# Squares of the attention sub-norm written to an SBUF tile instead of a PSUM bank, and seven statistics tiles with two buffers instead of three

## The chip, the cores and the metric

The kernel runs on one core of one Trainium2 chip. The metric is the device time of one execution in microseconds (us); less is better. Five engines run their own instruction streams, each in order, and meet at semaphores: TensorE (PE: matmuls and transposes, into PSUM), VectorE (DVE), ScalarE (ACT), GpSimd (POOL, which has no PSUM operand in this kernel) and SyncE (SP, which issues DMAs).

## The reference

A two-layer encoder over 1040 positions (1024 tokens and 16 meta tokens) with 1024 channels. Each layer computes, with `rms_norm(x, g) = x * rsqrt(mean(x*x) + eps) * g`:

```
h = rms_norm(h_res, norm_gain[li])
f_in, q, k, v, gate = split(h @ w_in[li])
f_out = real(fft2(f_in per group)) @ w_fourier          # 4 groups of 128 channels
q, k = rotary(rms_norm(q)), rotary(rms_norm(k))         # 4 heads, two maps of 64 channels each
o = (softmax(q0 k0) - lam * softmax(q1 k1)) @ v         # per head, 128 channels
o = rms_norm(o, subln_gain[li]) * (1 - lambda_init)     # the attention sub-norm
h_res = h_res + (concat(f_out, o) * silu(gate)) @ w_out
```

The sub-norm needs, for each position and head, the sum of the squares of 128 numbers. It is this sum that the change touches most.

## The kernel before, in words

All large products are split into a high and a low part (F32R), so one product takes three matmuls. A layer has four stages: the Fourier group (`fourier`, lines L352 to L450), the projection of head 0, attention, and the output projection (`out_fourier`, `phase_out`, matmuls of L286). Attention on one head needs little TensorE time beside its waits, so the projections of heads 1 to 3 (matmuls of L547) and later the output projection (L286) run inside it as a filler: a generator from which `fill(n)` takes steps.

Attention runs over 4 heads and, in each, 4 groups of query tiles: two tiles of 128 rows, in the last group of layer 0 also the 16 meta rows. For one tile (an item):

- `scores`: matmuls of L635 and L637 write the scores of one of the two maps into S, a PSUM tile of three banks of which there is one. DVE L642 copies the scores to SBUF (tile p) and finds the row's extreme, ACT L645 takes the exponential and its sum. The same for the second map. DVE L653 combines the two.
- `transposes`: eight transposes (L663, four to a bank) and one small one for the 16 meta columns (L670, a third bank) turn p around. ACT L667 and L673 copy the result out of PSUM, DVE L668 and L674 subtract to get the low part.
- `values`, after a group's last item: 25 matmuls (L682, L683) into one bank, copied to the SBUF tile osb by ACT L685.
- `finish`, one item later: TensorE transposes osb into a bank (L696, tile `pb`), ACT L698 copies it back over osb (`ot` is a view of osb), ACT L703 squares `ot` with the row scale r1 and sums the squares into `so`, writing the squares themselves back into the bank `pb`. DVE L705, POOL L707 (power -1/2) and DVE L708 make the row factor, DVE L710 multiplies it and the gate into gt, and SP sends it off.

The banks `pb` of `transposes`, `values`, `finish`, and those for keys (L587) and queries (L614), all come from one pool M of three PSUM banks (`psM`, tag "M"); S takes three banks and the pool G, for projections, two, which makes eight. A bank is free for its next user when the last instruction that reads or writes it is done. The squares of L703 are never read; only their sums are.

`wl`, the low part of a weight block, is made by POOL (in part by DVE) at L184 from the staged weights wst and the high part wh (ACT, L182).

The order of instructions on each engine is not that of the code: a list scheduler, with its own timing of the chip, orders them when the kernel is built, gives each tile a buffer of its pool and puts in the semaphore waits. `fill` sets the filler's priority below that of the attention work.

Of the kernel before, what the change touches and what calls it, by code (L numbers as in the profile page):

```python
# [10 lines left out]
F32 = mybir.dt.float32  # L11
F32R = mybir.dt.float32r
AF = mybir.ActivationFunctionType
# [5 lines left out]
P = 128  # L19
# [31 lines left out]
def trunk(ctx: ExitStack, tc, x, meta, ngain, w_in, w_f, qg, kg, lq1, lk1, lq2, lk2, subg, w_out,  # L51
          ident_d, chan_d, rope_d, dft_d, dftt_d, out, dbg=None):
    nc = tc.nc
    pe, act, dve, pool, sp = nc.tensor, nc.scalar, nc.vector, nc.gpsimd, nc.sync
# [4 lines left out]
    sm = ctx.enter_context(tc.tile_pool(name="sm", bufs=3))  # L59
# [7 lines left out]
    def nm(s):  # L67
        uid[0] += 1
        return f"{s}_{uid[0]}"
# [28 lines left out]
    def tile_rows(t):  # L98
        return NMETA if t == NT else P
# [113 lines left out]
    def norm_tile(hT, hM, gb, xt, t, wk, inplace=False):  # L213
        R, pos = tile_rows(t), P * t
        xn = wk.tile([P, D], F32, tag="xn", name=nm("xn"), bufs=1 if inplace else 2)
        ssq = sm.tile([P, 1], F32, tag="ssq", name=nm("ssq"))
        act.activation(xn[0:R], xt[0:R], AF.Square, accum_out=ssq[0:R])
        ms = sm.tile([P, 1], F32, tag="ms", name=nm("ms"))
        dve.tensor_scalar(ms[0:R], ssq[0:R], 1.0 / D, EPS, op0=ALU.mult, op1=ALU.add)
        rs = sm.tile([P, 1], F32, tag="rs", name=nm("rs"))  # L220
        pool.tensor_tensor(rs[0:R], ms[0:R], nhalf[0:R, 0:1], op=ALU.pow)
        if inplace:
            xn = xt
        dve.scalar_tensor_tensor(xn[0:R], xt[0:R], rs[0:R], gb[0:R], op0=ALU.mult, op1=ALU.mult)
        for c in range(2):
            pb = bank()
            for j in range(4):
                k = 4 * c + j
                pe.transpose(pb[:, R * j:R * j + R], xn[0:R, P * k:P * k + P], ident[0:R, 0:R])
            src = pb[:, 0:4 * R].rearrange("p (k r) -> p k r", k=4)  # L230
            hi = hT[:, 4 * c:4 * c + 4, 0, pos:pos + R]
            lo = hT[:, 4 * c:4 * c + 4, 1, pos:pos + R]
            act.copy(hi, src)
            dve.tensor_tensor(lo, src, f(hi), op=ALU.subtract)
            if t == NT:
                for o, part in ((0, hi), (32, lo)):
                    act.copy(hM[:, 4 * c:4 * c + 4, o:o + R], f(part))
# [218 lines left out]
    def head_projection(li, h, hT, hM, ep, wk, store, w, nxt, progress):  # L456
# [7 lines left out]
        ss = None  # L464

        def evacuate(t, ps, a, kv):
            nonlocal ss
            R = tile_rows(t)
            with tc.high_priority(EVAC):
                if t == NT:  # L470
                    pm = [ep.tile([P, 256], F32, tag="sq", name=nm("pm"), bufs=3) for _ in range(2)]
                    for part, u, v in ((pm[0], a, 256), (pm[1], 256, 384 if kv else 512)):
                        part = part[0:R, u % 256:(v - 1) % 256 + 1]
                        act.copy(part, ps[32:32 + R, u:v])
                        dve.tensor_tensor(part, ps[0:R, u:v], part, op=ALU.add)
                    pqk, pvg = pm[0], pm[1]
                else:
                    pqk, pvg = ps[:, 0:256], ps[:, 256:512]
                if not kv:
                    gs = ep.tile([P, P], F32, tag="gs", name=nm("gs"), bufs=2)  # L480
                    act.activation(gs[0:R], pvg[0:R, P:2 * P], AF.Tanh, scale=0.5)
                    dve.scalar_tensor_tensor(gs[0:R], gs[0:R], 1.0, pvg[0:R, P:2 * P], op0=ALU.add, op1=ALU.mult)
                act.copy(qk[0:R, t, a:256], pqk[0:R, a:256])
                sq = ep.tile([P, 256], F32, tag="sq", name=nm("sq"), bufs=3)
                act.activation(sq[0:R, a:256], pqk[0:R, a:256], AF.Square)
                act.copy(va[0:R, t, :], pvg[0:R, 0:P])
            if not kv:
                sp.dma_start(gtd[li][h][t, 0:R, :], gs[0:R])
            if t % 3 == 0:
                ss = sm.tile([P, 12], F32, tag="ss", name=nm("ss"))  # L490
            c0, c1 = 4 * (t % 3) + a // HD, 4 * (t % 3) + 4
            if t == NT:
                pool.memset(ss[:, 4 * (t % 3):c1], 1.0)
            dve.tensor_reduce(ss[0:R, c0:c1], sq[0:R, a:256].rearrange("p (c d) -> p c d", d=HD), axis=AX.X,
                              op=ALU.add)
            if t % 3 == 2:
                t0 = t - 2
                reg = qk[:, t0:t0 + 3, :]
                dve.tensor_scalar(ss, ss, 1.0 / HD, EPS, op0=ALU.mult, op1=ALU.add)  # L499
                rs = sm.tile([P, 12], F32, tag="rsq", name=nm("rsq"))  # L500
                pool.tensor_tensor(rs, ss, nhalf[:, 0:12], op=ALU.pow)  # L501
                n12 = reg.rearrange("p t (c d) -> p (t c) d", d=HD)
                dve.tensor_tensor(n12, n12, rs.unsqueeze(2).to_broadcast([P, 12, HD]), op=ALU.mult)
                n5 = reg.rearrange("p t (i c d) -> p (t i) c d", i=2, d=HD)

                def tab(x, lo, hi):
                    y = x[:, t0:t0 + 3, :, lo:hi].rearrange("p t i d -> p (t i) d")
                    return y.unsqueeze(2).to_broadcast([P, 6, 2, hi - lo])

                r1 = ep.tile([P, 256], F32, tag="sq", name=nm("r1"), bufs=3)  # L510
                r2 = ep.tile([P, 256], F32, tag="sq", name=nm("r2"), bufs=3)
                r1 = r1[:, 0:12 * ROT].rearrange("p (t c d) -> p t c d", t=6, c=2)
                r2 = r2[:, 0:12 * ROT].rearrange("p (t c d) -> p t c d", t=6, c=2)
                dve.tensor_tensor(r1, n5[:, :, :, 0:ROT], tab(cgt, 0, 16), op=ALU.mult)
                dve.tensor_tensor(r2[:, :, :, 0:8], n5[:, :, :, 8:16], tab(sgt, 0, 8), op=ALU.mult)
                dve.tensor_tensor(r2[:, :, :, 8:16], n5[:, :, :, 0:8], tab(sgt, 8, 16), op=ALU.mult)
                dve.tensor_tensor(n5[:, :, :, 0:ROT], r1, r2, op=ALU.add)
                progress[h] = t // 3 + 1
                if t == NT and ("qk", li, h) in dbg:
                    sp.dma_start(dbg["qk", li, h], qk)  # L520
# [35 lines left out]
    def attention(li, wk, store, fill, marks, ready, progress):  # L556
# [131 lines left out]
        def finish(h, gi, osb, ls):  # L688
            sets = [(0, 2, P)] + ([(2, 1, NMETA)] if len(group_tiles(gi)) > 2 else [])
            for i0, n, R in sets:  # L690
                t0 = group_tiles(gi)[i0]
                gt = wk.tile([P, 2, P], F32, tag="gt", name=nm("gt"), bufs=1)
                sp.dma_start(gt[0:R, 0:n], gtd[li][h][t0:t0 + n, 0:R, :].rearrange("t p d -> p t d"))
                pb = bank()
                for i in range(n):
                    pe.transpose(pb[0:R, P * i:P * i + P], osb[:, P * (i0 + i):P * (i0 + i) + R], ident)  # L696
                ot = osb[:, 0:2 * P].rearrange("p (t d) -> p t d", t=2)
                act.copy(ot[0:R, 0:n], pb[0:R, 0:P * n].rearrange("p (t d) -> p t d", t=n))  # L698
                r1 = sm.tile([P, 2], F32, tag="r1", name=nm("r1"))
                dve.reciprocal(r1[0:R, 0:n], ls[0:R, i0:i0 + n])  # L700
                so = sm.tile([P, 2], F32, tag="so", name=nm("so"))
                for i in range(n):
                    act.activation(pb[0:R, P * i:P * i + P], ot[0:R, i], AF.Square, scale=r1[0:R, i:i + 1],  # L703
                                   accum_out=so[0:R, i:i + 1])
                dve.tensor_scalar(so[0:R, 0:n], so[0:R, 0:n], 1.0 / P, EPS, op0=ALU.mult, op1=ALU.add)  # L705
                rs = sm.tile([P, 2], F32, tag="rso", name=nm("rso"))
                pool.tensor_tensor(rs[0:R, 0:n], so[0:R, 0:n], nhalf[0:R, 0:n], op=ALU.pow)  # L707
                dve.tensor_tensor(rs[0:R, 0:n], rs[0:R, 0:n], r1[0:R, 0:n], op=ALU.mult)  # L708
                for i in range(n):
                    dve.scalar_tensor_tensor(gt[0:R, i], ot[0:R, i], rs[0:R, i:i + 1], gt[0:R, i],  # L710
                                             op0=ALU.mult, op1=ALU.mult)
                    sp.dma_start(yad[li][t0 + i][0:R, P * h:P * h + P], gt[0:R, i])
                    if h == NH - 1:
                        ready.add(t0 + i)
# [29 lines left out]
        for n, item in enumerate(items):  # L744
            h, gi, i, t = item
# [107 lines left out]
    with tc.tile_pool(name="in0", bufs=2, side="right", reuse_waits="tile") as wk:  # L853
        for t in list(range(MT)) + [NT] + list(range(MT, NT)):
            R = tile_rows(t)
# [9 lines left out]
    for li in range(DEPTH):  # L865
# [9 lines left out]
        acm, wk = open_pool(f"at{li}", far, 2)  # L875
# [125 lines left out]
```

## Time and profile before

| | us |
|---|---|
| median of 3 runs | 1237.96 (1237.94 to 1243.18) |
| profiled execution, its own time | 1239.06 |
| its span on the page | 1236.9 |
| TensorE busy (matmuls) | 1169.6 (95%) |
| VectorE busy | 832.9 (67%) |
| ScalarE busy | 647.4 (52%) |
| GpSimd busy | 262.8 (21%) |
| the two attention stretches, about | 215 to 620 and 845 to 1210 |

The profile is of one execution; its own time lies 1.1 us above the median. Busy time says how long an engine had an instruction running; idle time before an instruction is put down to the engine and line whose end released it (`DVE atl L668`: the VectorE instruction of line 668 that writes atl). Where an instruction waits for several, the one that ended last is named.

### The profile page before, as it was taken

How to read it: one execution, taken by the hardware profiler on the slowest of the kernel's cores; microseconds unless marked ns; L12 is line 12 of the kernel's file. 1: busy time of each engine (PE TensorE's matmuls, PEld its weight loads, DVE VectorE, ACT ScalarE, POOL GpSimd, SP SyncE). 2: the span in 40 equal slices, each digit the busy share in tenths (PEclk: the TensorE clock that was granted, in tenths of full speed). 3: DMA queues.
4: the chain of work that ended last, by engine and by line, in shares of the span. 5: the costliest groups of instructions: out<-in, count | busy, mean ns of one | idle time of the engine just before them, and what ended most of it. 6: DMA issues, size and time to landing. Idle time of an engine off the chain costs nothing.

```text
span 1236.9 us, 18756 instructions
## 1 busy us (share of the span) xinstructions
PE 1169.6 (95%) x6676; PEld 1000.8 (81%) x6676; DVE 832.9 (67%) x1793; ACT 647.4 (52%) x1588; POOL 262.8 (21%) x231
## 2 busy tenths in 40 slices
PE   6999899989998998999999999999999999999998
PEld 6999786877777776778879998877878887878786
DVE  6352435777778778887775244557768888898863
ACT  6232325566657667566453323344667666766631
POOL 5111216023212213011012103252142121211200
PEclk9999899999999999999999999999999999999999
DMA  7420203012002004644436111120020020265353
GB/s 227 136 69 35 73 27 99 7 30 75 12 18 82 16 25 147 187 148 130 147 113 197 54 34 55 59 80 26 16 82 22 28 73 25 82 225 162 109 162 114
DMA packets 103612, 105.46 MB, mean 85 GB/s; under 512 B 11232, under 2 KB 87584, under 8 KB 103264
## 3 DMA queue, kind: packets, MB, share of 16 engines
q1 hardware_dynamic: 103104, 99.59, 25.9%
q0 software_dynamic: 416, 4.70, 1.1%
q8 instruction: 52, 0.85, 0.3%
q14 instruction: 40, 0.33, 0.1%
HBM read 74.62 MB, written 29.62 MB: 84 GB/s over the span
## 4 chain that ended last, share of the span: by engine, by line
PE 66%; DVE 12%; DMA 7%; ACT 6%; issue 5%; POOL 2%; SPq 1%; POOLq 0%; ACTq 0%; DVEq 0%
PE G L547 20%; PE G L286 10%; PE G L352 7%; PE S L352 6%; PE M L682 5%; PE S L635 4%; PE S L637 3%; PE S L547 3%; DVE p L642 3%; PE M L663 2%; PE M L393 2%; DMA wst<-in_w_in_dram 2%; ACT p L645 2%; DVE p L653 1%; DMA xt<-in_x_dram 1%
## 5 line engine op out<-in xcount | busy, mean ns | idle before, releaser
L547 PE MATMUL G<-wh,hT 128*128 128x512 f32 x896 | 308.7, 404 | 4.7 <-ACT wh L182 2.5
L645 ACT ACTIVATE p<-p,mx 128x1040 f32<-128x1040 f32 x136 | 158.4, 1165 | 99.7 <-DVE p L642 96.6
L547 PEld LDWEIGHTS G<-wh,hT 128*128 128x128 f32 x896 | 169.2, 190 | 44.6 <-ACT wh L182 3.4
L642 DVE TENSOR_SCALAR_CACHE_REDUCE p<-S 128x1040 f32<-128x1040 f32 x136 | 167.8, 1234 | 33.0 <-PE S L637 28.4
L547 PE MATMUL G<-wl,hT 128*128 128x512 f32 x448 | 178.2, 399 | 1.8 <-POOL wl L184 1.8
L184 POOL TENSOR_TENSOR wl<-wst,wh 128x512 fp32r<-128x512 f32 x82 | 112.6, 1384 | 235.7 <-ACT wh L182 131.1
L286 PE MATMUL G<-wh,yh 128*128 128x512 f32 (+2 forms) x276 | 107.8, 404 | 3.6 <-DVE xt L293 2.3
L182 ACT CAST wh<-wst 128x512 fp32r<-128x512 f32 x128 | 75.0, 620 | 65.0 <-DMA wst<-in_w_in_dram 22.2
L286 PE MATMUL G<-wl,yh 128*128 128x512 f32 (+2 forms) x276 | 106.6, 395 | 0.0
L501 POOL TENSOR_TENSOR rsq<-ss,nhalf 128x12 f32<-128x12 f32 x24 | 58.4, 2433 | 219.4 <-DVE ss L499 190.8
L547 PEld LDWEIGHTS G<-wl,hT 128*128 128x128 f32 x448 | 85.3, 190 | 18.1 <-POOL wl L184 2.8
L352 PE MATMUL G<-hT,wh 128*128 128x384 f32 (+3 forms) x384 | 96.4, 332 | 0.0
L286 PE MATMUL G<-wh,yl 128*128 128x512 f32 (+1 forms) x260 | 93.4, 400 | 0.0
L668 DVE TENSOR_TENSOR atl<-M,ath 128x512 fp32r<-128x512 f32 x136 | 87.0, 656 | 8.0 <-ACT ath L667 6.9
L352 PE MATMUL S<-hT,wh 128*128 128x256 f32 (+3 forms) x384 | 90.7, 320 | 1.0 <-DVE sg L440 1.0
L653 DVE SCALAR_TENSOR_TENSOR p<-p,cc,p 128x1040 f32<-128x1040 f32 (+1 forms) x68 | 89.2, 1312 | 1.5
L637 PE MATMUL S<-k,ql 128*128 128x264 f32 (+3 forms) x408 | 87.3, 321 | 0.0
L667 ACT CAST ath<-M 128x512 fp32r<-128x512 f32 x136 | 73.8, 561 | 22.0 <-PE M L663 21.2
L707 POOL TENSOR_TENSOR rso<-so,nhalf 128x2 f32<-128x2 f32 (+1 forms) x36 | 25.3, 702 | 273.6 <-DVE so L705 256.5
L663 PE MATMUL M<-ident,p 128*128 128x128 f32 x544 | 74.2, 270 | 7.4 <-ACT M L703 3.5
L184 DVE TENSOR_TENSOR wl<-wst,wh 128x512 fp32r<-128x512 f32 x46 | 44.4, 966 | 47.6 <-ACT wh L182 47.3
L663 PEld LDWEIGHTS M<-ident,p 128*128 128x128 f32 x544 | 61.6, 140 | 15.4 <-ACT M L703 4.4
(193 smaller groups left out, 2542.1 us busy)
## 6 DMA issues: line engine op xcount, KB each, us to landing
wst<-in_w_in_dram SPq DMA_DIRECT2D x64, 192.0 KB, 2.8
xt<-in_x_dram SPq DMA_DIRECT2D x16, 512.0 KB, 3.9
wst<-in_w_in_dram SPq DMA_DIRECT2D x32, 256.0 KB, 3.6
wst<-in_w_out_dram SPq DMA_DIRECT2D x16, 512.0 KB, 4.0
xmid<-xt SPq DMA_DIRECT2D x16, 512.0 KB, 3.3
xt<-xmid SPq DMA_DIRECT2D x16, 512.0 KB, 4.3
tab<-in_dft_dram POOLq DMA_DIRECT2D x2, 2096.0 KB, 10.0
yfd<-sg SPq DMA_DIRECT2D x8, 520.0 KB, 2.7
```

The costliest lines, as they stand in the source:

```text
L182: act.copy(h, self.staged[q][:, j, :])
L184: eng.tensor_tensor(l, self.staged[q][:, j, :], f(h), op=ALU.subtract)
L286: pe.matmul(pb[0:m, 0:e - c], lhsT=a[:, k, 0:m], rhs=b[2 * k + n][:, c:e], start=k == 0 and i == 0, stop=k == 3 and i == n_pass - 1)
L352: pe.matmul(o, lhsT=w[k][:, c:c + P], rhs=hT[:, k, s, a:b], start=k == 0 and i == 0, stop=k == KT - 1 and i == 2)
L547: pe.matmul(pss[t][0:part.shape[-1], a:b], lhsT=part, rhs=w[k][:, a:b], start=k == 0 and i == 0, stop=k == KT - 1 and i == len(pairs) - 1)
L637: ins = pe.matmul(ps[0:R, C0 + a:C0 + b], lhsT=ql[:, qo:qo + R], rhs=kk[:, a:b], start=False, stop=True)
L642: dve.tensor_scalar(pc[0:R], ps[0:R, C0:C0 + L], -1.0, None, op0=ALU.mult, op1=ALU.min, accum_out=mx[0:R])
L645: act.activation(pc[0:R], pc[0:R], AF.Exp, bias=mx[0:R], scale=-1.0, accum_out=lc)
L653: dve.scalar_tensor_tensor(pp[0][0:R], pp[1][0:R], cc[0:R], pp[0][0:R], op0=ALU.mult, op1=ALU.add)
L663: pe.transpose(pb[:, R * j:R * j + R], pa[0:R, P * kt:P * kt + P], ident[0:R, 0:R])
L667: act.copy(hi, src)
L668: dve.tensor_tensor(atl[:, 4 * c:4 * c + 4, qo:qo + R], src, f(hi), op=ALU.subtract)
```

## The change

The squares of the sub-norm go to a new SBUF tile `sqo` of 128 by 128 numbers with one buffer. The bank `pb` of `finish` is then last touched by the copy of L698. Seven small statistics tiles (ssq, ms, rs, ss, rsq, so, rso) are given two buffers where they had three. Lines after 701 move down by one: L703 becomes L704.

```diff
@@ norm_tile
-        ssq = sm.tile([P, 1], F32, tag="ssq", name=nm("ssq"))
+        ssq = sm.tile([P, 1], F32, tag="ssq", name=nm("ssq"), bufs=2)
         act.activation(xn[0:R], xt[0:R], AF.Square, accum_out=ssq[0:R])
-        ms = sm.tile([P, 1], F32, tag="ms", name=nm("ms"))
+        ms = sm.tile([P, 1], F32, tag="ms", name=nm("ms"), bufs=2)
         dve.tensor_scalar(ms[0:R], ssq[0:R], 1.0 / D, EPS, op0=ALU.mult, op1=ALU.add)
-        rs = sm.tile([P, 1], F32, tag="rs", name=nm("rs"))
+        rs = sm.tile([P, 1], F32, tag="rs", name=nm("rs"), bufs=2)
@@ evacuate, in head_projection
-                ss = sm.tile([P, 12], F32, tag="ss", name=nm("ss"))
+                ss = sm.tile([P, 12], F32, tag="ss", name=nm("ss"), bufs=2)
...
-                rs = sm.tile([P, 12], F32, tag="rsq", name=nm("rsq"))
+                rs = sm.tile([P, 12], F32, tag="rsq", name=nm("rsq"), bufs=2)
@@ finish, in attention
-                so = sm.tile([P, 2], F32, tag="so", name=nm("so"))
+                so = sm.tile([P, 2], F32, tag="so", name=nm("so"), bufs=2)
+                sqo = wk.tile([P, P], F32, tag="sqo", name=nm("sqo"), bufs=1)
                 for i in range(n):
-                    act.activation(pb[0:R, P * i:P * i + P], ot[0:R, i], AF.Square, scale=r1[0:R, i:i + 1],
+                    act.activation(sqo[0:R], ot[0:R, i], AF.Square, scale=r1[0:R, i:i + 1],
                                    accum_out=so[0:R, i:i + 1])
...
-                rs = sm.tile([P, 2], F32, tag="rso", name=nm("rso"))
+                rs = sm.tile([P, 2], F32, tag="rso", name=nm("rso"), bufs=2)
```

The scheduler makes another order of it. Up to the first `finish` of layer 0 all engines have the order of before. From there on the orders part, mostly inside layer 0's attention, in short pieces. Three places follow; a number behind a tile's name tells its copies apart, and the brackets name the engines whose semaphores a row waits for.

ScalarE in the first `finish`, before (osb_2373 is the group's output, M_2398 the bank of `finish`, M_2437, M_2444 and M_2451 those of the next item's transposes):

```order
L698 COPY osb_2373<-M_2398 128x256 [waits PE_49,Activation_49]
L667 CAST ath<-M_2437 128x4x128 [waits PE_49]
L667 CAST ath<-M_2444 128x4x128 [waits PE_49]
L703 ACTIVATE M_2398,so_2404<-osb_2373,r_342_2402 128x128 [waits Activation_49] x2
L673 CAST att<-M_2451 16x128 [waits PE_49]
L673 CAST att<-M_2451 16x128
```

and after:

```order
L698 COPY osb_2373<-M_2398 128x256 [waits PE_49,Activation_49]
L667 CAST ath<-M_2438 128x4x128 [waits PE_49]
L667 CAST ath<-M_2445 128x4x128 [waits PE_49]
L704 ACTIVATE sqo_2405,so_2404<-osb_2373,r_342_2402 128x128 [waits Activation_49]
L673 CAST att<-M_2452 16x128 [waits PE_49]
L673 CAST att<-M_2452 16x128
L704 ACTIVATE sqo_2405,so_2404<-osb_2373,r_342_2402 128x128 [waits Activation_49]
```

The squares write sqo, and the copies of the small transpose (L673) stand between the two of them.

TensorE around the second `finish` of layer 0, before (M_2678, M_2685 and M_2692 are the three banks of one item's transposes):

```order
L663 MATMUL M_2678<-ident,p_2497 128x128 [waits DVE_49]
L663 MATMUL M_2678<-ident,p_2497 128x128 x3
L635 MATMUL S_2736<-k_2058,qa_2532 128x264 [waits DVE_49]
L635 MATMUL S_2736<-k_2058,qa_2532 128x512
L635 MATMUL S_2736<-k_2058,qa_2532 128x264
L637 MATMUL S_2736<-k_2058,ql_2027 128x264
L637 MATMUL S_2736<-k_2058,ql_2027 128x512
L637 MATMUL S_2736<-k_2058,ql_2027 128x264
L663 MATMUL M_2685<-ident,p_2497 128x128 [waits DVE_49]
L663 MATMUL M_2685<-ident,p_2497 128x128 x3
L670 MATMUL M_2692<-ident,p_2497 16x128 [waits DVE_49]
```

and after:

```order
L663 MATMUL M_2680<-ident,p_2498 128x128 x4
L635 MATMUL S_2738<-k_2058,qa_2533 128x264 [waits DVE_49]
L635 MATMUL S_2738<-k_2058,qa_2533 128x512
L635 MATMUL S_2738<-k_2058,qa_2533 128x264
L637 MATMUL S_2738<-k_2058,ql_2027 128x264
L637 MATMUL S_2738<-k_2058,ql_2027 128x512
L637 MATMUL S_2738<-k_2058,ql_2027 128x264
L663 MATMUL M_2687<-ident,p_2498 128x128 [waits DVE_49]
L663 MATMUL M_2687<-ident,p_2498 128x128 x3
L670 MATMUL M_2694<-ident,p_2498 16x128 [waits Activation_49]
```

The order is the same, but the small transpose L670 waits for ScalarE and no longer for VectorE.

TensorE where the projection of head 2 of layer 0 begins, before (wh and wl are the two parts of its weight block, G_3055 and G_3058 the bank):

```order
L635 MATMUL S_2921<-k_2059,qb_2533 128x264
L637 MATMUL S_2921<-k_2059,ql_2028 128x264
L637 MATMUL S_2921<-k_2059,ql_2028 128x512
L637 MATMUL S_2921<-k_2059,ql_2028 128x264
L683 MATMUL M_2855<-att,vt 128x256 [waits DVE_49]
L547 MATMUL G_3055<-wh_2810,hT_150 128x512 [waits Activation_49]
L547 MATMUL G_3055<-wl_2811,hT_150 128x512 [waits Pool_49]
L547 MATMUL G_3055<-wh_2810,hT_150 128x512
```

and after:

```order
L663 MATMUL M_2784<-ident,p_2629 128x128 [waits DVE_49]
L663 MATMUL M_2784<-ident,p_2629 128x128 x3
L547 MATMUL G_3058<-wh_2812,hT_150 128x512 [waits DVE_49,Activation_49]
L547 MATMUL G_3058<-wl_2813,hT_150 128x512 [waits Pool_49]
L547 MATMUL G_3058<-wh_2812,hT_150 128x512
```

The first matmuls with the new weights stand one item earlier: before the two blocks of scores (S_2888 and S_2924), the small transpose of that item and the 24 value matmuls that precede them in the order of before.

## Rows read from the trace of the kernel before

**Rows 1.** The page, part 1: engine busy time, share of the span, instructions.

```profile
PE 1169.6 (95%) x6676; PEld 1000.8 (81%) x6676; DVE 832.9 (67%) x1793; ACT 647.4 (52%) x1588; POOL 262.8 (21%) x231
```

**Rows 2.** Chain that ended last, in order of time: start, length, what.

```profile
291.52 5.55 PE G L547 x24
```

**Rows 3.** Waits, whole span: who waited for whom, total, times, longest (us).

```profile
PE M L670 <- DVE atl L668: 9.5, 6, 3.2
PE M L670 <- ACT M L703: 9.3, 8, 2.0
...
PE S L635 <- DVE p L642: 4.5, 7, 1.4
...
PE M L663 <- ACT M L703: 3.5, 3, 1.7
...
ACT xn L217 <- DVE ms L219: 0.6, 1, 0.6
```

**Rows 4.** Timeline, first `finish`, all engines: start, length, instruction [idle before <- releaser].

```profile
251.63 0.35 ACT L698 COPY osb<-M 128x256 f32<-128x256 f32 x1
...
251.88 0.64 PE L637 MATMUL S<-k,ql 128*128 128x264 f32 x3
...
253.43 1.28 DVE L668 TENSOR_TENSOR atl<-M,ath 128x512 fp32r<-128x512 f32 x2
253.69 0.19 ACT L703 ACTIVATION_READ_ACCUMULATOR M<-osb,r 128x1 f32 x1
...
253.93 0.28 PE L670 MATMUL M<-ident,p 128*16 128x128 f32 x1 [1.41 <-ACT M L703]
...
254.70 1.23 DVE L642 TENSOR_SCALAR_CACHE_REDUCE p<-S 128x1040 f32<-128x1040 f32 x1
...
254.87 0.70 POOL L707 TENSOR_TENSOR rso<-so,nhalf 128x2 f32<-128x2 f32 x1 [23.88 <-DVE so L705]
```

**Rows 5.** Timeline of TensorE: five small transposes that waited.

```profile
276.80 0.29 PE L670 MATMUL M<-ident,p 128*16 128x128 f32 x1 [3.17 <-DVE atl L668]
...
355.45 0.28 PE L670 MATMUL M<-ident,p 128*16 128x128 f32 x1 [0.73 <-DVE atl L668]
...
476.01 0.28 PE L670 MATMUL M<-ident,p 128*16 128x128 f32 x1 [1.60 <-ACT M L703]
...
905.58 0.28 PE L670 MATMUL M<-ident,p 128*16 128x128 f32 x1 [1.24 <-DVE atl L668]
...
974.07 0.28 PE L670 MATMUL M<-ident,p 128*16 128x128 f32 x1 [0.48 <-ACT M L703]
```

**Rows 6.** Timeline of ScalarE, second `finish` of layer 0.

```profile
273.48 0.37 ACT L698 COPY osb<-M 128x256 f32<-128x256 f32 x1
...
274.70 0.40 ACT L703 ACTIVATE M<-osb,r 128x128 f32<-128x128 f32 x1
```

**Rows 7.** TensorE by stretch: length, busy (instructions), granted clock, DMA share, GB/s.

```profile
276.00:281.00 5.00, 4.20 (x12) 0.66 0.26 70
...
573.90:580.00 6.10, 6.09 (x21) 0.72 0.19 26
```

**Rows 8.** By stretch: length; PE, PEld, DVE, ACT, POOL busy; clock; DMA.

```profile
140.00:480.00 340.00, 317.35 (x1738) 259.60 (x1739) 243.36 (x561) 197.23 (x503) 79.51 (x67) 0.98 0.14 41
```

**Rows 9.** Groups by form: busy us, mean ns | idle before, releasers.

```profile
L182 ACT CAST wh<-wst 128x512 fp32r<-128x512 f32 x128 | 75.0, 620 | 65.0 <-DMA wst<-in_w_in_dram 22.2 <-PE G L352 18.4 <-PE G L547 11.3
...
L703 ACT ACTIVATE M<-osb,r 128x128 f32<-128x128 f32 x64 | 24.2, 378 | 1.3
...
L789 ACT ACTIVATE yh<-G,sgc 128x512 fp32r<-128x512 f32 x16 | 10.9, 683 | 16.8 <-PE G L785 16.5
...
L600 ACT CAST vh<-va 128x1024 fp32r<-128x1024 f32 x8 | 8.4, 1049 | 4.7 <-PE M L682 4.7
```

**Rows 10.** Timeline of TensorE where head 2's projection begins after the change.

```profile
286.46 0.71 PE L635 MATMUL S<-k,qa 128*128 128x264 f32 x3
```

**Rows 11.** Timeline of GpSimd: seventh low part of head 2's weights.

```profile
287.01 1.29 POOL L184 TENSOR_TENSOR wl<-wst,wh 128x512 fp32r<-128x512 f32 x1 [2.01 <-ACT wh L182]
```

## The prediction

> **What bounds the kernel now.** I read the page first. TensorE is busy for 1169.6 us of a span of 1236.9 [rows 1], and the chain that ended last runs through long stretches of its matmuls, such as 24 of L547 in 5.55 us, 0.23 us each [rows 2]. There is no other engine near it: in the larger part of layer 0's attention VectorE is busy for 243.4 of 340 us, 72% [rows 8]. So time is to be won almost only in the 67 us (1236.9 - 1169.6) in which TensorE stands still, and where its clock is granted below full.
>
> The list of waits says what it stands still for. Three entries have to do with the pool M of three banks: L670, the small transpose that takes an item's third bank, waited 9.3 us in 8 places for the squares L703 and 9.5 us in 6 places for VectorE's L668; L663 waited 3.5 us in 3 places for L703 [rows 3]. These 22.3 us are a third of all idle time of TensorE.
>
> The timeline of the first `finish` shows the mechanism. ScalarE has copied the bank out at 251.98 (251.63 + 0.35). TensorE ends its scores at 252.52 and wants the bank for L670, but gets it at 253.93, when the second square is read out (253.69 + 0.19) [rows 4]. It waited 1.41 us for squares that nobody reads.
>
> **The change part by part.** *The bank.* With the squares in SBUF the bank is free after L698. At the first `finish` that is 251.98, half a microsecond before TensorE comes: the wait goes whole. Of the 12.8 us (9.3 + 3.5) that end with L703 I take off two places, 1.60 and 0.48 us [rows 5], since in the new order L670 there waits for VectorE; what it costs there is open. 10.7 us are left.
>
> In four places the old order let L670 wait for L668, and the new one lets it wait for ScalarE: 3.17, 0.73 twice (once at 454.87) and 1.24 us, 5.9 in all [rows 5]. The order of the second `finish` shows it. TensorE came there at 273.63 (276.80 - 3.17) and L698 ended at 273.85 (273.48 + 0.37) [rows 6], so about 0.2 us of the 3.17 stay. Removable together: 10.7 + 5.9, or 16.6 us.
>
> How much of it holds is not in the trace. TensorE comes earlier, but VectorE does not where it works without a gap: after the first `finish` it goes from L668 (to 254.71) straight into L642 at 254.70 [rows 4], and L642 feeds the exponential whatever TensorE does. What then comes late is the next L635, which needs S from L642; it already waits 4.5 us in 7 places [rows 3]. If everything holds, 16.6 us; if VectorE set the pace wherever the two meet, nothing. I take two thirds, 11.1 us, nearer the upper end because VectorE has 28% of its time free in that stretch [rows 8].
>
> *The clock.* In two stretches the granted clock is below full: 0.66 on the mean over 5 us from 276, and 0.72 over 6.1 us from 573.9 [rows 7], a mix of the two levels of 1.2 and 2.4 GHz. Right before the first TensorE had stood still for 3.17 us [rows 5], right before the second for the longest wait for L703, 2.0 us [rows 3]. The lost time is 5 x 0.34 + 6.1 x 0.28 = 1.7 + 1.7 = 3.4 us. Both waits go, so I take 3.4 us back; 0 if something else makes TensorE pause there.
>
> *The squares themselves.* ScalarE's form from SBUF to SBUF with a scale and 128 columns is not in the trace. The form as it stands (to PSUM) takes 378 ns. From SBUF to SBUF a cast of 512 columns takes 620 and one of 1024 columns 1049, or 0.84 ns a column; 128 columns would be 620 - 384 x 0.84 = 298 ns without a scale. The form with a scale from PSUM to SBUF takes 683 at 512 columns, so 361 at 128 [rows 9]. Between 298 and 378 ns, 68 squares change by -5.4 to 0 us on an engine that is 58% busy (197 of 340 us [rows 8]). I take 361 and a value of 0 for the path, since the squares no longer hold a bank.
>
> The Trainium skill, page "ScalarE: Activation LUTs", section "Step-by-step: what each stage is for", says the opposite of a free move: ScalarE writes faster to PSUM than to SBUF, and PSUM is the destination to choose unless TensorE needs most of it. The page gives no figure. The two casts and the scaled form above do not bear the rule out for this size, and its own exception (TensorE needs the banks) is the case here.
>
> *The two squares of a pair* now write one tile, sqo, one after the other. Both rows wait for their own engine in the old order too, so this costs nothing.
>
> *Seven tiles with two buffers.* The next writer must now wait for the reader of two uses before instead of three. For `so` that reader is POOL L707, which ended at 255.57 (254.87 + 0.70) [rows 4], while the next squares come at 274.70 [rows 6]: 19 us of room, and POOL had idled 23.88 us for its input. For ssq the whole list has one wait of 0.6 us [rows 3]. I take 0; at worst such a wait stands once for each of the seven tiles on the path, 4 us.
>
> *The new order.* The scheduler shifts some short pieces, and each can make TensorE meet a thing that isn't ready. The clearest is the start of head 2's projection, one item earlier. In the old trace that place in the program is 286.46, where the item's scores begin [rows 10]; 19 matmuls at 0.23 us [rows 2] and one block of scores (1.0 us) lead from there to the first matmul with the seventh low part, so TensorE asks for it at 291.9, or at 287.5 if it has gained the 1.4 and 3.0 us of the two `finish` before. The low part is ready at 288.30 (287.01 + 1.29) [rows 11]: a wait between 0 and 0.8 us. There are six such weight blocks inside attention, three in a layer. I charge each at 0.6, near the upper end: 3.6 us.
>
> Sum: 11.1 + 3.4 - 3.6 = 10.9 us. From the profiled execution's 1239.06 us that gives 1228.2; the median of the runs is 1.1 lower, so 1227.
>
> **The rivals.**
> - *Taken back.* VectorE and ScalarE set the pace in the item of a `finish`, and the next wait for L642, L653 or L668 grows by most of what went. For it speaks VectorE's gapless run from 253.43 to 255.93 [rows 4]; against it that its 28% of free time lies in between. A third of the 16.6 stays, one of the two clock falls goes, and the new order costs its 3.6: 5.5 + 1.7 - 3.6 = 3.6, so 1234.
> - *Longer squares.* Writing to SBUF takes ScalarE longer than writing to PSUM. Priced with the largest step between two forms of 512 columns, 683 - 620 = 63 ns [rows 9], 68 squares are 4.3 us, all of it on the path if the second cast L667 waits behind them: 1227 + 4.3, or 1231. The forms of rows 9 speak against it. (It is what the rule of the Trainium skill named above would do.)
> - *Weights too late: slower.* TensorE runs ahead of ScalarE's and POOL's weight parts at all six blocks. Where it asks before the cast of the last part has begun, it waits for a whole cast and a whole subtraction, 0.62 + 1.29 = 1.9 us [rows 9, 11], and that pause, as long as the one before 573.9, brings a clock fall of 1.7 with it: 6 x 3.6 = 21.6 us, against 11.1 + 3.4 won. That ends 7.1 us above, at 1245. Four blocks would eat the gain, and all six are needed before it can be told from no change. Against it: POOL idles four fifths of its time [rows 1] and would move up with TensorE, whose matmuls free its wl buffers.
> - *The bank is not the last to come.* L698 itself stands in ScalarE's queue behind an exponential, and L670 finds the bank no earlier: 1238. Against it stand L698's ends at 251.98 and 273.85, before or within 0.2 us of TensorE's coming [rows 4 to 6].
>
> **How the numbers follow.** Forecast 0.60 (1219 to 1233), taken back 0.24, longer squares 0.05, slower 0.07, bank not last 0.04. If all 18.7 us (12.8 + 5.9) and the clock came back with no new wait it would be 1237.96 - 22.1 = 1216. The range of 1219 to 1240 leaves out the best of this and the slower rival. Half a percent, 6.2 us, is about what can be told from no change here: faster means below 1231.8 and takes nearly all of the forecast, the better part of the longer squares and the lucky edge of "taken back", 0.64; slower 0.07; the rest 0.29.
>
> **What would show it.** In the profile of the changed kernel no wait of TensorE for the squares' line (now L704) may be left; waits of L670 and L663 for L698 should be below 1 us in all; those of L670 for L668 fall from 9.5 to about 4. The granted clock is full around 276 and 574. The squares take 340 to 380 ns. TensorE's busy time falls by the 3.4 us or so, its idle time by 7 to 8. If L635's wait for L642 (4.5) grows by as much as the others shrink, it was taken back; if waits of L547 or L286 for wl or wh grow past 10 us, the new order decided. The forecast is wrong if the bank waits are gone and the time is still above 1233.

## The result, and the profile after

The changed kernel takes 1223.17 us, the median of four runs (1219.01 to 1224.20), against 1239.51 for the kernel before (four runs); the ratio is 0.9865, with a 95% interval of 0.9845 to 0.9884. Run again with the second group of experiments, it took 1219.20 against 1239.11, ratio 0.9835 (0.9808 to 0.9862). It is faster by 16 to 20 us, where 10.9 were forecast; both medians lie inside the range of 1219 to 1240, 4 and 8 us below the 1227 us that were forecast. Of all executions of this document one alone, the profiled one of pool_qcopy, ran at a mean granted clock of 0.849 in place of some 0.99, in 1294.63 us, and it is left out of the medians.

The profiled execution took 1219.01 us, 20.05 less than the profiled one of before, so the two profiles lie further apart than the medians. Part 1 of the page of the changed kernel:

```profile
span 1217.2 us, 18766 instructions
...
PE 1163.7 (96%) x6676; PEld 998.2 (82%) x6676; DVE 834.8 (69%) x1793; ACT 645.2 (53%) x1588; POOL 265.2 (22%) x231
```

TensorE stands still for 53.5 us (1217.2 - 1163.7) in place of 67.3 [rows 1]: 13.8 us less, where 7 to 8 were forecast. Its busy time fell by 5.9 us with the same 6676 instructions. That goes with the granted clock: its mean is 0.991 in the profile of before and 0.997 in this one. The list of waits of the changed kernel (waiting instruction, releaser, total us, times, longest):

```profile
PE M L670 <- DVE atl L668: 6.6, 6, 1.4
PE S L635 <- DVE p L642: 4.1, 7, 0.9
...
PE M L229 <- DVE hT L234: 2.6, 3, 1.5
PE G L547 <- ACT wh L182: 2.6, 2, 1.7
PE G L547 <- ACT va L486: 2.5, 2, 2.2
PE G L547 <- POOL wl L184: 1.8, 2, 0.9
...
PE M L663 <- ACT osb L698: 0.5, 2, 0.2
...
PE M L670 <- ACT osb L698: 0.4, 2, 0.2
```

No entry names the squares any more. Their 12.8 us [rows 3] have become 0.9 us for the copy L698, the last reader of the bank now, and the waits of L670 for L668 went from 9.5 to 6.6. L635's wait for L642, where the time would have shown if VectorE had taken it back, went from 4.5 to 4.1. The timeline of the changed kernel shows the first two `finish` (start, length, engine, instruction, [idle before <- releaser]):

```profile
249.23 0.35 ACT L698 COPY osb<-M 128x256 f32<-128x256 f32 x1
...
249.49 0.63 PE L637 MATMUL S<-k,ql 128*128 128x264 f32 x3
...
249.95 0.27 PE L670 MATMUL M<-ident,p 128*16 128x128 f32 x1
...
250.44 0.42 ACT L704 ACTIVATE sqo<-osb,r 128x128 f32<-128x128 f32 x1
...
251.03 0.69 DVE L668 TENSOR_TENSOR atl<-M,ath 128x512 fp32r<-128x512 f32 x1
...
251.36 0.40 ACT L704 ACTIVATE sqo<-osb,r 128x128 f32<-128x128 f32 x1
...
251.63 1.23 DVE L642 TENSOR_SCALAR_CACHE_REDUCE p<-S 128x1040 f32<-128x1040 f32 x1
...
270.75 0.28 PE L670 MATMUL M<-ident,p 128*16 128x128 f32 x1 [0.17 <-ACT osb L698]
```

L670 follows the scores without idle time (249.95) where it had waited 1.41 us, and in the second `finish` it waits 0.17 in place of 3.17 [rows 4, 5]. It now runs ahead of both squares, and VectorE takes L642 right behind the first L668; before, L642 came behind both [rows 4].

### The profile page after: what moved, and what is told of

Its sections match the earlier page's. It is cut to its first block, busy times and chain, and to the rows that moved or that the text cites. A ratio compares the mean times of both kernels' runs of the same rounds, so it can differ in the third digit from the quotient of the medians.

```text
span 1217.2 us, 18766 instructions
## 1 busy us (share of the span) xinstructions
PE 1163.7 (96%) x6676; PEld 998.2 (82%) x6676; DVE 834.8 (69%) x1793; ACT 645.2 (53%) x1588; POOL 265.2 (22%) x231
## 4 chain that ended last, share of the span: by engine, by line
PE 66%; DVE 14%; DMA 6%; issue 5%; ACT 5%; POOL 3%; SPq 1%; POOLq 0%; ACTq 0%; DVEq 0%
PE G L547 19%; PE G L286 10%; PE G L352 6%; PE M L682 6%; PE S L352 6%; PE S L635 4%; PE S L637 4%; PE S L547 3%; DVE p L642 3%; PE M L663 2%; DMA wst<-in_w_in_dram 2%; PE M L393 2%; DVE p L653 2%; POOL wl L184 2%; DVE atl L668 2%
## 5 line engine op out<-in xcount | busy, mean ns | idle before, releaser
L547 PE MATMUL G<-wh,hT 128*128 128x512 f32 x896 | 307.2, 402 | 6.0 <-ACT wh L182 2.6
L547 PEld LDWEIGHTS G<-wh,hT 128*128 128x128 f32 x896 | 168.2, 189 | 46.2 <-ACT va L486 3.6
L642 DVE TENSOR_SCALAR_CACHE_REDUCE p<-S 128x1040 f32<-128x1040 f32 x136 | 167.7, 1233 | 30.4 <-PE S L637 23.2
L547 PE MATMUL G<-wl,hT 128*128 128x512 f32 x448 | 177.2, 397 | 1.8 <-POOL wl L184 1.8
L547 PEld LDWEIGHTS G<-wl,hT 128*128 128x128 f32 x448 | 84.7, 189 | 18.1 <-POOL wl L184 2.9
L501 POOL TENSOR_TENSOR rsq<-ss,nhalf 128x12 f32<-128x12 f32 x24 | 55.0, 2292 | 202.8 <-DVE ss L499 182.3
L668 DVE TENSOR_TENSOR atl<-M,ath 128x512 fp32r<-128x512 f32 x136 | 86.5, 655 | 6.9 <-ACT ath L667 5.8
L663 PE MATMUL M<-ident,p 128*128 128x128 f32 x544 | 73.0, 270 | 2.0 <-DVE atl L668 0.8
L682 PE MATMUL M<-ath,vh 128*128 128x256 f32 (+1 forms) x256 | 72.9, 285 | 0.8 <-DVE atl L668 0.8
```

Of the source, the lines that this page charges most:

```text
L547: pe.matmul(pss[t][0:part.shape[-1], a:b], lhsT=part, rhs=w[k][:, a:b], start=k == 0 and i == 0, stop=k == KT - 1 and i == len(pairs) - 1)
L642: dve.tensor_scalar(pc[0:R], ps[0:R, C0:C0 + L], -1.0, None, op0=ALU.mult, op1=ALU.min, accum_out=mx[0:R])
L663: pe.transpose(pb[:, R * j:R * j + R], pa[0:R, P * kt:P * kt + P], ident[0:R, 0:R])
L668: dve.tensor_tensor(atl[:, 4 * c:4 * c + 4, qo:qo + R], src, f(hi), op=ALU.subtract)
L682: pe.matmul(po[:, 0:w], lhsT=v[:, kt, :], rhs=a[:, kt, 0:w], start=kt == 0 and i == 0, stop=False)
```

## The experiments

The ratios below are to the kernel before, run beside it on the same chip.

**Only the buffers (bufs_only).** The squares stay in the bank:

```diff
-        ssq = sm.tile([P, 1], F32, tag="ssq", name=nm("ssq"))
+        ssq = sm.tile([P, 1], F32, tag="ssq", name=nm("ssq"), bufs=2)
...
-                so = sm.tile([P, 2], F32, tag="so", name=nm("so"))
+                so = sm.tile([P, 2], F32, tag="so", name=nm("so"), bufs=2)
```

> Only the seven statistics tiles get two buffers; the squares stay in their PSUM bank. Theory (the bank's release is the gain): the bank is still held until the second square, so TensorE's waits for the squares' line stay at 11 to 14 us and the time is that of before, 1237 to 1241 us; the squares stay near 378 ns. Rival 'any new order would have done it' (the scheduler's reshuffle and not the bank brings the time): the order differs from before, so the time may fall by 5 us or more, with the waits for the squares still there. Rival 'the smaller buffers cost something': 1242 or more, with new waits of DVE or ScalarE for ssq, ms, rs, ss or so.

1238.49 us (12 runs), ratio 0.9997 (0.9982 to 1.0012). The order of instructions is that of before on every engine, and so are the waits:

```profile
PE M L670 <- DVE atl L668: 9.5, 6, 3.1
PE M L670 <- ACT M L703: 9.3, 8, 2.0
...
PE M L663 <- ACT M L703: 3.5, 3, 1.7
```

The buffers neither cost nor bring anything, and they do not move the order.

**The squares in SBUF, but read from the bank (read_bank).** Against the changed kernel:

```diff
-                    act.activation(sqo[0:R], ot[0:R, i], AF.Square, scale=r1[0:R, i:i + 1],
+                    act.activation(sqo[0:R], pb[0:R, P * i:P * i + P], AF.Square, scale=r1[0:R, i:i + 1],
```

> As the changed kernel, but the squares read the bank itself instead of the copy in osb, and write to sqo in SBUF: the result of the squares leaves the bank, yet the bank is still held until the last square has read it. It computes the same. Theory (release of the bank): the waits of L670 and L663 for the squares come back, 10 us or more, and the time goes back to 1234 to 1242 us. Rival 'destination' (what helps is that ScalarE no longer writes into PSUM, or shorter squares): the time stays at 1219 to 1227. Rival 'new order': the order of the instructions is near that of the changed kernel, so 1219 to 1230 too.

1239.13 us (12 runs), ratio 1.0001 (0.9987 to 1.0016): the whole gain is gone, although ScalarE writes to sqo as in the changed kernel. The waits of this kernel:

```profile
PE M L670 <- ACT sqo L704: 11.5, 12, 1.9
...
PE S L635 <- DVE p L642: 6.2, 8, 1.4
PE M L670 <- DVE atl L668: 4.7, 5, 1.8
PE G L786 <- DMA ya<-yad: 4.7, 1, 4.7
PE M L663 <- ACT sqo L704: 2.8, 3, 1.4
```

The waits for the squares are back with 14.3 us. So it is not the destination that helped: where the bank is held, TensorE waits for it. One entry grew beside it: 4.7 us for a DMA, 0.9 before. The windows of this kernel from the last two `finish` of layer 0 to that wait's end (length, TensorE's busy time, instructions, clock, DMA):

```profile
583.72:618.15 34.43, 33.22 (x186) 1.00 0.39 136
618.15:630.15 12.00, 7.28 (x41) 0.92 0.20 67
```

and those of the kernel before:

```profile
589.95:620.55 30.60, 30.09 (x170) 1.00 0.37 132
620.55:632.21 11.66, 10.75 (x56) 1.00 0.20 69
```

From the last `finish` to the product that needs its rows back from memory it is 12 us in both. In read_bank the scheduler has put some 3 us of TensorE's work (33.22 against 30.09) ahead of that `finish`, and the work is then missing to cover the trip (7.28 against 10.75). This part of its time belongs to the order, not to the hold.

**The squares alone, in bfloat16, with three buffers (sqo16_three), and the changed kernel in bfloat16 (sqo16_two).** The first against the kernel before, the second has the same tile and the seven two-buffer edits:

```diff
+                sqo = wk.tile([P, P], BF16, tag="sqo", name=nm("sqo"), bufs=1)
...
-                    act.activation(pb[0:R, P * i:P * i + P], ot[0:R, i], AF.Square, scale=r1[0:R, i:i + 1],
+                    act.activation(sqo[0:R], ot[0:R, i], AF.Square, scale=r1[0:R, i:i + 1],
```

> The squares go to an SBUF tile in bfloat16 (half the room, so it fits without the smaller buffers), and all statistics tiles keep three buffers: the one half of the change without the other. The squares' values are read by nobody; the sums come from the accumulator in float32. Theory (release of the bank): no wait for the squares, 1219 to 1227 us, and squares of 380 to 415 ns. Rival 'the two buffers matter': the time differs from the changed kernel by more than 4 us. Rival 'new order': scatter of 5 us or more around the changed kernel although the waits for the squares are gone.

> The changed kernel with the squares' tile in bfloat16 instead of float32, nothing else. Theory: the bank goes free as early, 1219 to 1227 us; it also shows whether the 29 ns that the squares got longer hang on four bytes a column (then about 390 ns or less) or on SBUF as the destination at all (then 400 to 410). Rival 'new order': a spread of 5 us or more against the changed kernel, from places of the weight blocks or other details of the order.

1222.35 us, ratio 0.9875 (0.9851 to 0.9899), and 1218.78, ratio 0.9844 (0.9820 to 0.9868), five runs each. The half with the squares brings the gain by itself. Both kernels have the order of the changed kernel on every engine, line by line, so the new order, too, comes with the squares and not with the buffers. The 3.6 us between the two are not waits: TensorE's idle time is 51.1 and 54.3 us, smaller in the slower one. They are mostly clock: the mean share of the granted clock below full, times the span, is 8.6 us over the runs of the first and 5.8 over those of the second. The same four bytes or two, the squares take the same, as the groups by form show (columns: busy us, mean ns | idle before). The changed kernel:

```profile
L704 ACT ACTIVATE sqo<-osb,r 128x128 f32<-128x128 f32 x64 | 26.1, 407 | 1.4
```

sqo16_two:

```profile
L705 ACT ACTIVATE sqo<-osb,r 128x128 bf16<-128x128 f32 x64 | 26.0, 407 | 1.4
```

read_bank, whose squares come from PSUM:

```profile
L704 ACT ACTIVATE sqo<-M,r 128x128 f32<-128x128 f32 x64 | 24.3, 380 | 0.2
```

Against 378 ns from SBUF to PSUM [rows 9]: the square is 27 to 29 ns longer only where both sides are in SBUF, and the width of the result does not matter. (The reading of the accumulator behind it takes 194 ns, but 209 where the square reads PSUM.)

**The changed kernel again (after_again).** No edit.

> The changed kernel once more, as it is, so that the next three stand beside it on one chip. 1219 to 1225 us; the granted clock falls below full in places that the first profile of it did not show (near 142 or 812, where TensorE pauses for 2 to 2.6 us), or the first profile's clean stretches there were no accident of one execution.

1219.20 us (four runs), ratio 0.9835 (0.9808 to 0.9862); idle time 54.3 us (span 1216.6, busy 1162.3). The clock is taken up below.

**Half of the hold (half).** Against the changed kernel, the first square of a pair goes to the bank:

```diff
-                    act.activation(sqo[0:R], ot[0:R, i], AF.Square, scale=r1[0:R, i:i + 1],
+                    act.activation(pb[0:R, 0:P] if i < n - 1 else sqo[0:R], ot[0:R, i], AF.Square, scale=r1[0:R, i:i + 1],
```

> As the changed kernel, but of each pair the first square goes to the bank and only the second to sqo, so the bank is held one square (about 0.6 us) instead of two beyond the copy. It computes the same. Theory (release of the bank): the cost of the hold is made of waits of 0.7 to 2 us that end with the last square; with half the hold each such wait loses about 0.6 us, so of 12.8 us in 11 places some 5 to 7 stay, and the time is 1227 to 1233. Rival 'all or nothing' (any hold costs the whole, because the scheduler places L670 after the squares): 1235 or more. Rival 'taken back' (a part of the hold is hidden by VectorE anyway): 1219 to 1225, with waits for L668 instead.

1243.55 us (12 runs), ratio 1.0032 (1.0018 to 1.0047). My theory missed by over 10 us. The rival "all or nothing" had the time, but not the waits, which are a part and not the whole. The waits of this kernel:

```profile
PE S L635 <- DVE p L642: 8.7, 10, 2.8
PE M L670 <- DVE atl L668: 7.6, 8, 1.4
PE M L670 <- ACT M L704: 6.7, 8, 1.6
PE G L786 <- DMA ya<-yad: 4.8, 1, 4.8
...
PE M L663 <- ACT M L704: 2.0, 2, 1.2
...
PE M L587 <- ACT M L704: 0.5, 1, 0.5
```

The waits for the squares did shrink, to 9.2 us (6.7 + 2.0 + 0.5) from 12.8 in the kernel before and 14.3 in read_bank. But L635's waits for L642 grew to 8.7, where before has 4.5, L670's for L668 are 7.6, where read_bank has 4.7, and the uncovered DMA stands here too. By its waits this looks like the prediction's rival "taken back": a shorter hold that did not pay. In a table, in us (bank: all waits for the squares or for L698; idle: span less TensorE's busy time):

| kernel | bank | L670 on L668 | L635 on L642 | DMA ya | sum | idle |
|---|---|---|---|---|---|---|
| before | 12.8 | 9.5 | 4.5 | 0.9 | 27.7 | 67.3 |
| read_bank | 14.3 | 4.7 | 6.2 | 4.7 | 29.9 | 69.2 |
| half | 9.2 | 7.6 | 8.7 | 4.8 | 30.3 | 71.7 |
| changed | 0.9 | 6.6 | 4.1 | 0 | 11.6 | 53.5 |

The sum follows the idle time within 3 us, the bank column alone does not. How much of the time of half and read_bank is the hold as it runs and how much the order that the scheduler makes around it, these runs do not separate: bufs_only alone has the order of before, the two bfloat16 kernels alone that of the changed kernel, and read_bank and half have orders of their own. Free of TensorE's order the release can be read at the first `finish`, up to which that order is the same before and after: 1.41 us less of waiting there, of which 0.76 come back one item later, behind L668. At the second, with 19 rows in other places between the two, it is 3.00 us less.

**Each square twice (sq_twice).**

```diff
-                    act.activation(sqo[0:R], ot[0:R, i], AF.Square, scale=r1[0:R, i:i + 1],
-                                   accum_out=so[0:R, i:i + 1])
+                    for _ in range(2):
+                        act.activation(sqo[0:R], ot[0:R, i], AF.Square, scale=r1[0:R, i:i + 1],
+                                       accum_out=so[0:R, i:i + 1])
```

> As the changed kernel, with each square issued twice in a row (the second overwrites the first, the sums are the same): 68 more activations of about 407 + 193 ns, 40.8 us more of ScalarE, off the bank. Theory (the squares are off the path once they hold no bank): the time moves by 0 to 6 us, 1219 to 1229, so that the 29 ns by which a square got longer (2 us over all) cost at most 0.3 us. Rival 'longer squares': ScalarE is the bound in the item of a finish, all of it comes to the end of the kernel, 1255 to 1264 us.

1225.23 us (five runs), ratio 0.9882 (0.9853 to 0.9910), 6.0 us over the changed kernel beside it. Some 40 us more of ScalarE (68 x (402 + 189) ns by its groups) brought 6.0, or 0.15 us for each: as expected, at the upper end. At this rate the 29 ns of the longer squares, 2 us over 68, are worth an estimated 0.3. Where the 6.0 went, in its waits:

```profile
PE S L635 <- DVE p L642: 7.5, 10, 2.3
PE M L670 <- DVE atl L668: 7.2, 7, 1.6
```

These grew from 4.1 and 6.6 us: what reaches TensorE comes by way of VectorE. This kernel, too, has an order of its own, so how much of the 6.0 is the squares' own time is not shown.

**Read-outs at a higher priority (evac_first).**

```diff
-                act.copy(hi, src)
-                dve.tensor_tensor(atl[:, 4 * c:4 * c + 4, qo:qo + R], src, f(hi), op=ALU.subtract)
+                with tc.high_priority(EVAC):
+                    act.copy(hi, src)
+                    dve.tensor_tensor(atl[:, 4 * c:4 * c + 4, qo:qo + R], src, f(hi), op=ALU.subtract)
```

> The changed kernel with the read-out of the two transposed banks (ScalarE's copy L667 and VectorE's subtraction L668) put at the priority of the other evacuations, aimed at the 6.6 us that L670 still waits for L668. Theory: the waits of L670 for L668 fall below 3 us and up to 4 us come off, 1216 to 1222. Rival 'VectorE's own pace': what L668 gains, L642 loses; the waits of L635 for L642 grow from 4.1 us by as much, 1221 to 1230. Rival 'order': the read-outs move but little and the time is that of the changed kernel within 2 us.

1220.28 us (four runs), ratio 0.9846 (0.9818 to 0.9873), 1.1 from the changed kernel: the rival "order" had it. TensorE's order differs from that of the changed kernel at 13 of 6676 places, and the wait it was aimed at is untouched:

```profile
PE M L671 <- DVE atl L669: 6.6, 6, 1.4
```

**The queries' copy on GpSimd (pool_qcopy).**

```diff
-                dve.tensor_copy(dst[o, 0:w], f(dst[s, 0:w]))
+                pool.tensor_copy(dst[o, 0:w], f(dst[s, 0:w]))
```

> The changed kernel with the copies L621 of the queries (64 of about 289 ns, 18.5 us of VectorE) moved to GpSimd, which idles 78% of its time. Theory (what is left of the bank's waits, L670 behind L668 with 6.6 us and L635 behind L642 with 4.1, is VectorE's pace): 2 to 5 us come off these waits, 1215 to 1218 us. Rival 'latency': a copy on GpSimd takes longer than 289 ns and the scores wait for qa in 16 groups; L635's wait for L621 grows past 5 us and the time is 1222 or more. Rival 'order': VectorE is not what decides there, 1218 to 1222 with the waits as they are.

1227.47 us over five runs, ratio 0.9903 (0.9885 to 0.9921): 4 to 8 us slower than the two medians of the changed kernel, which were taken beside other runs, though relieving VectorE was to help. Its one profile is that at a clock of 0.849, so its waits aren't compared; GpSimd's copies took 462 and 418 ns in it, where VectorE's take 290 and 287. The time falls on the side of the rival "latency", but by which wait is open.

**The small transpose first (meta_first).** L670 and its read-out are issued ahead of the two L663:

```diff
+            pb = bank()
+            ins = pe.transpose(pb[0:NMETA, 0:R], pa[0:R, SEQ:L], ident[0:R, 0:R])
...
             for c in range(2):
                 pb = bank()
...
-            pb = bank()
-            ins = pe.transpose(pb[0:NMETA, 0:R], pa[0:R, SEQ:L], ident[0:R, 0:R])
```

> The changed kernel with the small transpose L670 and its read-out issued ahead of the two large ones L663, so that the large ones take the second and the third bank. Theory (the waits of L670 are those of whoever takes an item's third bank, not of the small transpose): the 6.6 us for L668 go over to L663, and the time stays within 3 us of the changed kernel, 1217 to 1223. Rival 'the small one in front pays': it asks first and its bank was free all along, the waits go, 1213 to 1217. Rival 'worse': the large transposes come later by the small read-outs (three short instructions), the values wait for atl, 1223 to 1230.

1266.18 us (five runs), ratio 1.0222 (1.0202 to 1.0242), far beyond what even the rival "worse" allowed. Its longest wait at the scores:

```profile
PE S L635 <- DVE p L642: 36.1, 29, 3.5
```

and its small subtraction among the groups by form:

```profile
L664 DVE TENSOR_TENSOR att<-M,att 16x128 fp32r<-16x128 f32 x64 | 17.9, 280 | 12.5 <-ACT att L663 10.7
```

Of the 6.6 us for the third bank 0.2 are left. But VectorE now stands idle for 12.5 us ahead of this subtraction of 280 ns (2.1 in the changed kernel), 10.7 of it for ScalarE; what follows in VectorE's order waits with it, and the scores wait for L642 with 36.1 us. That the first brings the second is argued: the whole order is another, and how 12.5 us become 36.1 is not shown. No version here beats the changed kernel by more than the intervals.

## Why the prediction was right, step by step

*The bank* was forecast at 11.1 us, two thirds of 16.6. The list gives 22.3 [rows 3] less 7.5 (6.6 + 0.5 + 0.4), so 14.8. The mechanism was right, and read_bank shows that it depends on when the bank's last reader is done. But what went and what came back I had placed wrongly. There are 68 small transposes, and counted in order they can be set side by side. Of the six that waited for L668 before, none does any more, not even those of 1.80 and 1.82 us that I had left standing, and the two for the squares that I had taken off (1.60 and 0.48) wait for nothing. The six waits of now, 6.6 us, are new: 0.76 us at 259.17, 1.13 at 325.98 and at 422.68, 1.35 at 472.26, 0.85 at 518.64 and 1.38 at 1030.64, all at transposes that did not wait for L668 before. Two neighbours (the tenth and the eleventh of the 68) in the kernel before:

```profile
332.28 0.28 PE L670 MATMUL M<-ident,p 128*16 128x128 f32 x1
...
342.93 0.28 PE L670 MATMUL M<-ident,p 128*16 128x128 f32 x1 [1.80 <-DVE atl L668]
```

and in the changed kernel, with one more of the new waits:

```profile
325.98 0.28 PE L670 MATMUL M<-ident,p 128*16 128x128 f32 x1 [1.13 <-DVE atl L668]
...
334.61 0.27 PE L670 MATMUL M<-ident,p 128*16 128x128 f32 x1
...
472.26 0.28 PE L670 MATMUL M<-ident,p 128*16 128x128 f32 x1 [1.35 <-DVE atl L668]
```

So all of the 22.3 us went, not 16.6, and 7.5 came back, at L668 and L698 and nothing at L642. I had argued the two thirds from VectorE's gapless run after the first `finish`, but that run belonged to the old order; in the new one L642 comes between the two L668. That 14.8 is two thirds of 22.3 is luck.

*The new order* was charged with 3.6 us at six weight blocks. The waits of L547 for wh and wl are 4.4 us (2.6 + 1.8), and were 4.3 (2.5 for wh, 1.8 for wl), and all of them stand outside the two attention stretches: nothing at the blocks. All other changes of idle time come to 1.0 us on balance (14.8 - 13.8). L229's waits for hT grew most, from 0.7 to 2.6, and L547's for va (L486) from 1.3 to 2.5; against them went L663's 1.8 for k and 1.2 for att. This term was mis-sized by about 2.6 us, and the bank's by 3.7; together they are 6.3 of the 5 to 9 us by which the forecast fell short.

*The clock* was forecast to give 3.4 us back. The windows of the changed kernel (length, TensorE's busy time, instructions, granted clock, DMA):

```profile
140.00:150.00 10.00, 7.93 (x39) 1.00 0.21 60
270.00:280.00 10.00, 9.53 (x52) 1.00 0.36 103
370.00:380.00 10.00, 7.85 (x36) 0.83 0.46 140
470.00:480.00 10.00, 7.80 (x43) 0.83 0.76 225
...
560.00:570.00 10.00, 9.07 (x58) 1.00 0.50 171
...
810.00:820.00 10.00, 7.22 (x30) 1.00 0.48 138
```

The kernel before, where it is below full outside [rows 7]:

```profile
140.00:150.00 10.00, 7.89 (x29) 0.66 0.18 53
...
830.00:840.00 10.00, 9.20 (x28) 0.66 0.24 69
```

The changed kernel a second time:

```profile
140.00:150.00 10.00, 8.94 (x37) 0.83 0.21 60
...
370.00:380.00 10.00, 7.86 (x35) 0.83 0.44 140
470.00:480.00 10.00, 7.65 (x48) 1.00 0.78 222
```

The two falls that I named are gone: the transposes of 276.80 and 573.91 now stand at 270.75 and 558.20, and the clock is full behind them. But it now falls near 375, behind the 2.15 us that L547 waits for va there, and near 472 in one execution of two. The new order did have a price, then, at a place and of a kind that I had not charged. At two more places, 142 and 830, the change does not reach what TensorE waits for (2.60 us for L440; 1.75 and 0.86 for wh and wl, and 1.71 and 0.85 now, at 813). The fall stands there in the profile of before with 3.4 us each, and at neither in the first one of after. That makes 6.8 us of the 20.05 between the two profiles; the two falls that I named and the new ones cancel, 3.4 against 3.4. What is left over many runs: the share below full times the span is 9.5 us on the mean of 51 runs of before, and 6.4 on that of eight of the changed kernel (7.9 in the first four, 4.9 in the other four). So about 3.1 us came back. That the size agrees with the forecast is in part luck, since new falls took back some of what I had counted.

*The squares* were the wrong step in kind: 361 ns forecast, 407 measured, 29 longer than to PSUM instead of 17 shorter. The Trainium skill, page "ScalarE: Activation LUTs", section "Step-by-step: what each stage is for", had this right (ScalarE writes faster to PSUM than to SBUF). From a source in SBUF the traces agree with it, 378 against 407 ns. I had set it aside on casts of 512 columns and more and on a form that reads PSUM. read_bank shows why that form misled: a square that reads PSUM takes 380 ns to SBUF as well. I had priced the longer squares at up to 4.3 us; sq_twice puts them at about 0.3. The exception that the Trainium skill makes, PSUM that TensorE needs, decided.

*The two squares of a pair* and *the seven tiles* at 0: right, shown for the tiles by bufs_only.

The sum with the measured terms, the waits of one profile each and the clock over many runs, is 14.8 + 3.1 - 1.0 = 16.9 us, against 16.3 and 19.9 by the two pairs of medians. Of the rivals, "the bank is not the last to come" and "weights too late" have nothing for them (0.9 us for L698, 0.1 more at the weights), "longer squares" is true and nearly free, and "taken back" happened for a third of the waits (7.5 of 22.3), not for the two thirds that it was priced at.

## What to carry to other kernels

Ask of every scratch result in a PSUM bank how long it keeps the bank after its last useful reader; what it may cost stands in the list of waits under the line that holds it, and moving the scratch may pay even where the engine writes it more slowly. Compare the waits one by one, and not only their totals: 6.6 us that seem to have stayed here were all new. Shortening a hold need not pay: cut to half here, its waits shrank and the time did not, whether for the rest of the hold or for the order around it. Before moving a tiny instruction forward, read what it would wait for, since an engine that works in order has everything else behind it.

## What the runs showed of the hardware that I had not expected

A square with a scale and an accumulated sum of 128 columns takes 378 ns from SBUF to PSUM, 380 from PSUM to SBUF and 407 from SBUF to SBUF, the last in float32 and bfloat16 alike (402 in meta_first, 403 in sq_twice).

The same pause does not always bring the same clock. At about 142 us TensorE has stood still for 2.6 us in each of the eleven profiles used here, behind the same instruction, and the mean granted clock from 140 to 150 us was 1.00 in one of them, 0.83 in six and 0.66 or 0.67 in four; two executions of one kernel gave 1.00 and 0.83. So two single profiles can differ by some 3 us at one place without any change there.
